# One quarter of the gate stage's input: transposed by DMA through DRAM in place of TensorE

## The chip, the cores and the metric

The kernel runs on one core of a Trainium2 chip. The core has five engines that run their own instruction streams and wait for one another by semaphores: TensorE (PE in the profile: matmuls and transposes into PSUM; PEld is its loading of the stationary operand), VectorE (DVE), ScalarE (ACT), GpSimd (POOL) and SyncE (SP), which here only issues DMAs. DMAs issued by SyncE and by GpSimd run on the same 16 DMA engines. The metric is the device time of one execution in microseconds. A measurement is the median of several executions.

## The reference

One layer of a transformer trunk on 512 tokens of width 2048, all in float32: a sliding-window attention mixer, then a gated embedding, then a norm. Cut to what matters here:

```python
x = x + swa_mixer(rmsnorm(x, norm_g), ...)      # attention, ends with (out * silu(gate)) @ w_out
emb = p @ ple_proj                              # [512, 256] @ [256, 2048]
g = sigmoid(rmsnorm(x, ple_norm) @ ple_gate)    # [512, 2048] @ [2048, 2048]
x = x + emb * g
return rmsnorm(x, final_g)
```

The change concerns the step from the second line's left side to the third: x, which lies with tokens on partitions, must be turned so that its 2048 columns lie on partitions, because a matmul contracts over partitions. The columns are scaled by `ple_norm` on the way. The mean square of each token enters later, as a scale of the sigmoid's input.

## The kernel before

Float32 products are made from three matmuls each (`mm3`, lines 126 to 128): both operands are split into a rounded high part and the rest, and high x high, low x high and high x low are added. The high part of a weight piece is a cast on ScalarE (line 729), the low part a subtraction on VectorE (line 730). So one weight piece of 128 x 1024 is loaded (L722, on SyncE; L709 on GpSimd where it is added to what is there), cast, subtracted, and then used by twelve matmuls.

The last two matrix products of the layer, the output projection (stage "o", with `w_out`) and the gate (stage "g", with `ple_gate`), are each made as seven products of half-size blocks instead of eight (a Strassen scheme; in the output stage one of the seven is itself made of seven smaller ones). `ORDER_OUT` = (1, 7, 6, 5, 3, 4) and `ORDER_PLE` = (2, 7, 1, 6, 5, 3, 4) give the order of the products. Each product p has two halves jj of its columns, and each half (a call of `unit`) four steps m: a step takes one weight piece, gives out a share of the list `later` (additions into x, squares), calls `todo()` and then `between(m)`, which handles the smaller products. The forms (sums of quarters of the left operand, split in high and low) of the next product are made beside the current one by the generator `nxt`; those of the first gate product by `ple_first`.

`x1[j]` is column block j (512 columns) of x, with tokens on partitions, t = 0 to 3 counting blocks of 128 tokens. `add_to_x` adds a product to a block and counts in `missing` how many additions are still due; with the last one it calls `squares(t, j)`. The blocks with t >= 2 and j >= 2, the lower right quarter of x, get their last addition from product 5.

`hT[g]` is column block g of the turned x: 128 partitions, 4 blocks of 128 columns, 512 tokens. `turn(kp, th, tag)` turns the column blocks 2kp and 2kp + 1 for one half th of the tokens: four TensorE transposes of 128 x 128 into one PSUM bank (L1023), then two multiplications by `ple_norm` on ScalarE into `hT` (L1026). There are 16 such turns. Twelve are spread over the steps of the last output product (p = 4), in this order: the columns 1024 to 2047 for tokens 256 to 511, the same columns for tokens 0 to 255, the columns 0 to 1023 for tokens 0 to 255. The last four (columns 0 to 1023, tokens 256 to 511) stand in the first gate product. The lower right quarter (`hT[2]` and `hT[3]`, tokens 256 to 511) is needed first by the forms of gate product 6, which are made beside product 1.

What sets the order: TensorE's and SyncE's instructions run as the program lists them; from the second gate product on those of all engines do. Before that, the order on ScalarE, VectorE and GpSimd is a scheduler's. SyncE's loads follow the rule in `Pieces.ahead`: a piece is asked for 6 pieces ahead in the output stage (from product 6 on), 3 or 4 in the gate stage, and each load waits in SyncE's queue until its buffer is free. `pT` (L1168), an operand of the embedding product, is loaded after the output stage into a buffer of the weight pieces, cast at L1169 and subtracted at L1170.

The `quarter` buffers (four of them) hold the attention gates first and `hT` afterwards. The tile `partial` (two buffers) holds intermediate results `s2` and `s7` of the gate stage.

Of the kernel before, what the change touches and what calls it, by code (L numbers as in the profile page):

```python
# [10 lines left out]

F32 = mybir.dt.float32
F32R = mybir.dt.float32r
AF = mybir.ActivationFunctionType
ALU = mybir.AluOpType
AX = mybir.AxisListType
# [4 lines left out]
P = 128  # L21
# [34 lines left out]
def trunk_kernel(ctx: ExitStack, tc: tile.TileContext, a: dict):  # L56
    nc = tc.nc
# [12 lines left out]
    pn = const.tile([P, KC], F32, name="pn")  # L70
# [8 lines left out]
    def quarter(name):  # L79
        return whole.tile([P, 4, S], F32, tag="quarter", name=name)  # L80
# [7 lines left out]
    class Weights:  # L88
# [15 lines left out]
        def _make(self, i):  # L104
            self.load(min(i + 2, len(self.srcs)))
            raw = self.raw[i]
            hi = wpool.tile([P, WE], F32R, tag="whi", name=f"whi{i}")
            lo = wpool.tile([P, WE], F32R, tag="wlo", name=f"wlo{i}")
            nc.scalar.copy(hi, raw)  # L109
# [48 lines left out]
    def run(gen):  # L158
        for _ in gen:
            pass  # L160
# [34 lines left out]
    for k in range(KC):  # L195
# [25 lines left out]
        h = room.tile([P, S], F32R, tag="ah", name=f"xh{k}")  # L221
# [41 lines left out]
        f, e = k == 0, k == KC - 1  # L263
# [18 lines left out]
        for part in "hl" if f else "lh":  # L282
            for t in range(NB):
                c = slice(t * P, (t + 1) * P)
# [6 lines left out]
        if 3 <= k < 3 + NB:  # L291
            t = k - 3
# [110 lines left out]
    for b in range(exact, BUCKETS):  # L403
        d = np.nonzero(bk == b)[0]
        if len(d):
            lo, n = P - 1 + int(d.min()), len(d)
# [130 lines left out]
    def turn(i):  # L537


        d, g = divmod(i, UNITS)  # L540
        pr = T.pop(i)
        pt = bank(f"pt{i}", "t")[:, :256]
        for u in range(2):
            nc.tensor.transpose(pt[:, u * P : (u + 1) * P], pr[:, u, :], ident)  # L544

        j, part = divmod(i, 2)
        if part == 0:
            own = None
            if g >= P // TQ:
                own = apool.tile([P, 2, S], F32R, tag="own", name=f"own{j}")  # L550
            PT[j] = apool.tile([P, 2, S], F32R, tag="r", name=f"r{j}"), own
        r, own = PT[j]
        rh, rl = (r[:, l].rearrange("p (h t u q) -> p t u h q", h=GROUP, t=2, u=2)[:, part] for l in range(2))
        src = pt.rearrange("p (u h q) -> p u h q", u=2, h=GROUP)
        nc.scalar.copy(rh, src)  # L555
        nc.vector.tensor_sub(rl, src, rh.bitcast(F32))  # L556
        yield
        b = j % 2
        flat = lambda v, rows: v[rows].rearrange("p l (h t q) -> p t (l h) q", h=GROUP, t=2)[:, part]
        if own is not None:  # L560
            rows = slice(0, P) if b else slice(0, HB)
            sign = -1 if b else 1
            nc.gpsimd.affine_select(  # L563
                out=flat(own, rows), in_=flat(r, rows).bitcast(F32), pattern=[[0, 2 * GROUP], [sign, TQ]],
                compare_op=ALU.is_ge, fill=0.0, base=(-HB - 1 if b else 0) + sign * part * TQ, channel_multiplier=-sign,
            )
        yield
        if own is not None:
            here, there = slice(HB, P), slice(0, HB)
            if not b:  # L570
                here, there = there, here
            nc.scalar.copy(flat(own, there)[:, :GROUP], flat(own, here)[:, GROUP:].bitcast(F32))
# [98 lines left out]
    for (nm, p), small in zip(SUMS, (7, 5, 6, 4, None, None)):  # L671
        for m in range(2 if small else 0):
            t = summed["small", small, m] = tc.dram_tile([P, WE], F32, name=f"small_{small}_{m}")
# [5 lines left out]
        for jj in range(2):  # L679
            for m in range(4):  # L680
                t = summed[nm, p, jj, m] = tc.dram_tile([P, WE], F32, name=f"{nm}_{p}_{jj}_{m}")
# [223 lines left out]
    for i in range(blocks + 3):  # L905

        before, softmax = softmax, scores(i) if i < blocks else iter(())
        turned = turn(i - 2) if 2 <= i < blocks + 2 else iter(())
# [48 lines left out]
    x1 = [x1s[:, j] for j in range(4)]  # L957
# [46 lines left out]
    def partial(nm):  # L1004
        return late.tile([P, 2, 2, 512], F32, tag="partial", name=nm, bufs=2)

    def squares(t, j):
        junk = late.tile([P, 512], F32, tag="junk", name=f"junk{j}_{t}", bufs=3)
        nc.scalar.activation(junk, x1[j][:, t, :], AF.Square, accum_out=ssq2[:, t, j : j + 1])

    hT = {}

    def turn(kp, th, tag):

        g = kp // 2
        if g not in hT:
            hT[g] = quarter(f"hT{g}")
        tp = bank(f"tp{kp}_{th}", tag)
        for n in range(2):
            k = 2 * kp + n  # L1020
            for tb in range(2):
                src = x1[k // 4][:, 2 * th + tb, (k % 4) * P : (k % 4 + 1) * P]
                nc.tensor.transpose(tp[:, (2 * n + tb) * P : (2 * n + tb + 1) * P], src, ident)  # L1023
        for n in range(2):
            k = 2 * kp + n
            nc.scalar.mul(hT[g][:, k % 4, th * 256 : th * 256 + 256], tp[:, n * 256 : n * 256 + 256], pn[:, k : k + 1])  # L1026
# [9 lines left out]
    def add_to_x(j, t, sign, ps):  # L1036
        xt = x1[j][:, t, :]
        if sign > 0:
            nc.vector.tensor_add(xt, ps, xt)
        else:  # L1040
            nc.vector.tensor_sub(xt, xt, ps)
        missing[j, t] -= 1
        if not missing[j, t]:
            squares(t, j)


    halves = [gates[2 + h][:, :, :256].rearrange("p k (r t) -> p r k t", r=2) for h in range(2)]
# [67 lines left out]
    turns = []  # L1115
# [7 lines left out]
    for n, p in enumerate(ORDER_OUT):  # L1123
        nxt = out_forms.steps(ORDER_OUT[n + 1]) if n < 5 else iter(())
        for jj in range(2):
            later.extend(held.pop(waiting.get((p, jj)), ()))
            calls = iter(range(4))

            def between(m):
                q = small_steps.get((p, jj, m))  # L1130
                if q is not None:
                    next(small_made.setdefault(q, small_form(q)))
                q = SMALL.get((p, jj), {}).get(m)
                if q is not None:
                    small(q)

            def todo():
                step = next(calls)
                part = x_at.get((p, jj, step))
                if part is not None:  # L1140
                    load_x(part, nc.sync)
                next(nxt, None)
                if p == 4:

                    for _ in range({0: 1, 1: 2, 2: 2, 3: 2, 5: 1, 6: 2, 7: 2}.get(4 * jj + step, 0)):
                        turn(*turns.pop(0), "o")
                    if jj:
                        next(ple_first, None)

            ps = unit(p, jj, at_out, out_forms, todo, between)  # L1150
            posts = [partial_of(add_y, p, jj, tb, ps[tb]) for tb in range(2)]
            if p == 1:
                held[p, jj] = posts
            else:
                later.extend(posts)
        run(nxt)
        if p == 3:
            nc.sync.dma_start(fg, a["final_g"].partition_broadcast(P))
        if p == 3:
            turns = [(kp, th) for kp0, th in ((4, 1), (4, 0), (0, 0)) for kp in range(kp0, kp0 + 4)]  # L1160
    run(ple_first)
    assert not turns

# [51 lines left out]
    turns = [(kp, 1) for kp in range(4)]  # L1215
# [36 lines left out]
    early = {(5, 0, 3): 0, (5, 1, 1): 1, (5, 1, 3): 2, (3, 0, 1): 3, (3, 0, 3): 4, (3, 1, 1): 5, (3, 1, 3): 6}  # L1252
# [10 lines left out]
    for n, p in enumerate(ORDER_PLE[:-1]):  # L1263
        if n == 1:

            ctx.enter_context(
                tc.manual_schedule(
                    engines={getattr(mybir.EngineType, v) for v in ("PE", "SP", "DVE", "Activation", "Pool")}
                )
            )  # L1270
        nxt = ple_forms.steps(ORDER_PLE[n + 1])
        for jj in range(2):
            calls = iter(range(4))

            def todo():
                k = early.get((p, jj, next(calls)))
                if turns:
                    turn(*turns.pop(0), "s")
                    if not turns:
                        nc.vector.tensor_reduce(ss2, ssq2, axis=AX.X, op=ALU.add)  # L1280
                        run(rsqrt_mean(rstd2, ss2, D, "r2"))
                    return
                next(nxt, None)
                if p == 2:
                    next(nxt, None)
                if k is not None:
                    split_last(k)

            ps = unit(p, jj, at_ple, ple_forms, todo)
            e = {}  # L1290
            if p in (1, 5, 3):
                w = B.get(at_ple[p, jj][3] + 1)
                for t in (0, 1) if p in (1, 3) else (2, 3):
                    e[t] = embed(t, w, "to"[jj])
            if (p, jj) != (3, 1):
                later.insert(0, partial_of(gate_later, p, jj, ps, e))
            if (p, jj) == (5, 1):
                later.extend(moved.pop())
        run(nxt)
# [5 lines left out]
    f = ple_forms.made[4]  # L1305
# [31 lines left out]
    g = block(0, 0, "s", "o")()  # L1337
# [12 lines left out]
    g = block(1, 0, "s", "t")()  # L1350
# [10 lines left out]
    g = block(0, 1, "p", "o")()  # L1361
# [13 lines left out]
    g = block(1, 1, "p", "t", slice(0, 256))()  # L1375
# [4 lines left out]
    n = done[3]  # L1380
# [87 lines left out]
```

## Time and profile before

| | us |
|---|---|
| median of 3 executions | 792.71 (791.97 to 794.43) |
| profiled execution | 792.22 |
| its span, first to last instruction | 790.4 |
| TensorE busy | 780.8 |
| VectorE busy | 590.9 |
| ScalarE busy | 517.3 |
| GpSimd busy | 141.0 |

The span is the time between the first and the last instruction of the profiled execution; the time of an execution lies somewhat above it. A busy time is the sum of the time in which an engine had an instruction in work. In 40 equal slices of the span (19.8 us each), the digits are tenths of busy time; PEclk is the clock that TensorE was granted, DMA the mean busy share of the 16 DMA engines:

```profile
PE   9999999999999999999999999999999999999995
...
ACT  6735368776877676766666654456699656656765
POOL 0030222333332313341333100000000120210000
PEclk9999999999999999999999999999999999999998
DMA  8787977999999989899878499667864996787633
```

The output stage ends and the gate stage begins about the 31st slice; the turns lie between 572.6 and 619 us.

### The profile page before, as it was taken

The numbers are of one execution on the slowest core, as the hardware profiler recorded it, in microseconds if no ns is written. First come the engines' busy times: TensorE is split into PE (matmuls) and PEld (weight loads), VectorE is DVE, ScalarE is ACT, GpSimd is POOL, SyncE is SP. The second block draws the span as 40 slices with busy tenths as digits, with TensorE's granted clock in tenths as the row PEclk, the third lists the DMA queues.
The fourth block names the chain that finished last, engine by engine and source line by source line (L and its number), as shares of the span: only waits on it lengthen the run. The fifth ranks groups of instructions, "written<-read, shape, count | busy, mean of one in ns | idle before, by whom it ended". The sixth has DMA issues, their size and how long they took to land.

```text
span 790.4 us, 11177 instructions
## 1 busy us (share of the span) xinstructions
PE 780.8 (99%) x3658; PEld 649.2 (82%) x3658; DVE 590.9 (75%) x1171; ACT 517.3 (65%) x1131; POOL 141.0 (18%) x252
## 2 busy tenths in 40 slices
PE   9999999999999999999999999999999999999995
PEld 7888888888888888888888888888888888888885
DVE  4537568877888678776777899778867757988896
ACT  6735368776877676766666654456699656656765
POOL 0030222333332313341333100000000120210000
PEclk9999999999999999999999999999999999999998
DMA  8787977999999989899878499667864996787633
GB/s 337 244 213 253 297 192 229 291 265 291 251 253 282 242 229 263 215 254 252 228 201 184 137 371 342 190 217 233 273 235 142 348 206 198 157 227 218 182 106 107
DMA packets 44618, 184.87 MB, mean 234 GB/s; under 512 B 6720, under 2 KB 7232, under 8 KB 39440
## 3 DMA queue, kind: packets, MB, share of 16 engines
q1 hardware_dynamic: 36480, 142.94, 52.0%
q0 software_dynamic: 8080, 41.22, 27.4%
q8 instruction: 29, 0.48, 0.2%
q14 instruction: 29, 0.24, 0.1%
HBM read 177.26 MB, written 62.97 MB: 304 GB/s over the span
## 4 chain that ended last, share of the span: by engine, by line
PE 98%; DMA 0%; DVE 0%; ACT 0%; issue 0%; ACTq 0%; SPq 0%; DVEq 0%
PE gps L126 7%; PE gps L127 7%; PE gps L128 7%; PE qps L126 7%; PE qps L127 7%; PE qps L128 7%; PE o L128 6%; PE g L128 6%; PE g L126 6%; PE o L126 6%; PE g L127 5%; PE o L127 5%; PE s L476 2%; PE o L584 2%; PE vps L286 2%; PE pt L544 2%
## 5 line engine op out<-in xcount | busy, mean ns | idle before, releaser
L730 DVE TENSOR_TENSOR blo<-braw,bhi 128x1024 fp32r<-128x1024 f32 x102 | 124.5, 1223 | 41.0 <-ACT bhi L729 40.5
L729 ACT CAST bhi<-braw 128x1024 fp32r<-128x1024 f32 x102 | 107.4, 1053 | 72.8 <-PE o L128 26.4
L126 PE MATMUL gps<-xh,whi 128*128 128x512 f32 x256 | 100.5, 393 | 0.0
L127 PE MATMUL gps<-xl,whi 128*128 128x512 f32 x256 | 100.0, 391 | 0.0
L128 PE MATMUL gps<-xh,wlo 128*128 128x512 f32 x256 | 99.8, 390 | 0.0
L126 PE MATMUL qps<-xh,whi 128*128 128x512 f32 x224 | 87.6, 391 | 0.0
L127 PE MATMUL qps<-xl,whi 128*128 128x512 f32 x224 | 87.5, 391 | 0.0
L128 PE MATMUL qps<-xh,wlo 128*128 128x512 f32 x224 | 87.2, 389 | 0.0
L110 DVE TENSOR_TENSOR wlo<-wraw,whi 128x1024 fp32r<-128x1024 f32 x60 | 74.3, 1239 | 13.1 <-ACT whi L109 12.4
L126 PE MATMUL g<-bhi,fhg 128*128 128x512 f32 x192 | 75.1, 391 | 0.0
L126 PE MATMUL o<-bhi,fho 128*128 128x512 f32 x192 | 74.8, 390 | 0.0
L128 PE MATMUL g<-bhi,flg 128*128 128x512 f32 x192 | 74.8, 389 | 0.0
L128 PE MATMUL o<-bhi,flo 128*128 128x512 f32 x192 | 74.7, 389 | 0.0
L127 PE MATMUL g<-blo,fhg 128*128 128x512 f32 x192 | 74.7, 389 | 0.0
L127 PE MATMUL o<-blo,fho 128*128 128x512 f32 x192 | 74.7, 389 | 0.0
L555 ACT CAST r<-pt 128x256 fp32r<-128x256 f32 x64 | 23.9, 373 | 74.6 <-PE pt L544 74.5
L556 DVE TENSOR_TENSOR r<-pt,r 128x256 fp32r<-128x256 f32 x64 | 27.1, 423 | 57.2 <-ACT r L555 56.9
L109 ACT CAST whi<-wraw 128x1024 fp32r<-128x1024 f32 x60 | 62.3, 1039 | 10.6 <-PE qps L127 5.9
L563 POOL TENSOR_SCALAR_AFFINE_SELECT own<-r 64x512 fp32r<-64x512 f32 (+1 forms) x48 | 34.4, 718 | 167.0 <-PE o L587 80.7
L491 POOL COPY t<-sinkb 128x2 f32<-128x2 f32 x64 | 41.2, 644 | 99.3 <-ACT pr L533 38.7
L128 PEld LDWEIGHTS gps<-xh,wlo 128*128 128x128 f32 x256 | 48.1, 188 | 10.3
L126 PEld LDWEIGHTS gps<-xh,whi 128*128 128x128 f32 x256 | 48.1, 188 | 8.9
(230 smaller groups left out, 1753.5 us busy)
## 6 DMA issues: line engine op xcount, KB each, us to landing
w_out<-in_w_out POOLq DMA_DIRECT2D x32, 512.0 KB, 8.1
wraw<-in_w_gate_in SPq DMA_DIRECT2D x32, 512.0 KB, 6.8
braw<-w_out SPq DMA_DIRECT2D x32, 512.0 KB, 4.7
wraw<-in_w_q SPq DMA_DIRECT2D x28, 512.0 KB, 7.3
braw<-in_ple_gate SPq DMA_DIRECT2D x24, 512.0 KB, 3.6
braw<-in_w_out SPq DMA_DIRECT2D x22, 512.0 KB, 4.3
xw<-in_first SPq DMA_DIRECT2D x14, 640.5 KB, 6.5
w_out<-in_w_out SPq DMA_DIRECT2D x16, 512.0 KB, 11.2
```

Of the source, the lines that this page charges most:

```text
L109: nc.scalar.copy(hi, raw)
L110: nc.vector.tensor_sub(lo, raw, hi.bitcast(F32))
L126: nc.tensor.matmul(ps, sh, mh, start=first, stop=False, skip_group_check=more)
L127: nc.tensor.matmul(ps, sh, ml, start=False, stop=False, skip_group_check=more)
L128: nc.tensor.matmul(ps, sl, mh, start=False, stop=last, skip_group_check=more)
L286: nc.tensor.matmul(v_ps[t], h[:, c], part_of(high_at, 256, 512), start=f, stop=e, skip_group_check=True)
L491: nc.gpsimd.tensor_copy(two(0, W + W - 1 if late else W, 1), sinkb[:, d : d + 1].unsqueeze(1).to_broadcast([P, 2, 1]))
L555: nc.scalar.copy(rh, src)
L556: nc.vector.tensor_sub(rl, src, rh.bitcast(F32))
L563: nc.gpsimd.affine_select(out=flat(own, rows), in_=flat(r, rows).bitcast(F32), pattern=[[0, 2 * GROUP], [sign, TQ]], compare_op=ALU.is_ge, ...
L729: nc.scalar.copy(hi, raw)
L730: nc.vector.tensor_sub(lo, raw, hi.bitcast(F32))
```

## The change

The lower right quarter of x no longer goes through TensorE. Its four blocks of 128 tokens x 512 columns go another way:

- `apart(t, j)`, called right after a block's squares: GpSimd copies the block, seen as 16 bit halves, so that the lower halves of a row come first and the upper halves behind them, into a `partial` tile, and a DMA of GpSimd's queue stores it in DRAM (`halves_of`).
- `cross(t, j)`, called at steps 1 and 3 of both halves of output product 4: SyncE issues one transposing DMA that reads those 256 rows of 512 halves and writes them into `hT[j]`, so that the two halves of each value meet again side by side.
- `crossed(kp)`, at the four steps of the first half of gate product 7: ScalarE multiplies the eight column blocks by `ple_norm` in place.

The four turns of that quarter are gone. The other eight turns of output product 4 keep their steps; steps 0 and 1 have none any more, and step 2 has one in place of two. The four turns in the first gate product stay.

```diff
+    def turned(g):
         if g not in hT:
             hT[g] = quarter(f"hT{g}")
+        return hT[g]
+
+    halves_of = [tc.dram_tile([2 * P, 2, 512], U16, name=f"halves_of{n}") for n in range(2)]
+    parts_of, crossings = [], []
+
+    def apart(t, j):
+
+        if not parts_of:
+            parts_of.append(partial("apart").rearrange("p a b c -> p (a b c)").bitcast(U16))
+        n = len(crossings)
+        to = parts_of[0][:, 1024 * n : 1024 * n + 1024].rearrange("p (h c) -> p h c", h=2)
+        nc.gpsimd.tensor_copy(to, x1[j][:, t, :].bitcast(U16).rearrange("p (c h) -> p h c", h=2))
+        nc.gpsimd.dma_start(halves_of[j - 2][(t - 2) * P : (t - 1) * P], to)
+        crossings.append((t, j))
+
+    def cross(t, j):
+
+        to = turned(j).rearrange("p k t -> p (k t)").bitcast(U16).rearrange("p (k t) -> p k t", k=4)
+        rows = halves_of[j - 2][(t - 2) * P : (t - 1) * P].rearrange("t h c -> (t h) c")
+        nc.sync.dma_start_transpose(to[:, :, t * 2 * P : (t + 1) * 2 * P], rows)
+
+    def crossed(kp):
+        for k in (2 * kp, 2 * kp + 1):
+            part = hT[kp // 2][:, k % 4, 256:]
+            nc.scalar.mul(part, part, pn[:, k : k + 1])
...
@@ def add_to_x
         if not missing[j, t]:
             squares(t, j)
+            if t >= 2 and j >= 2:
+                apart(t, j)
...
@@ todo of the output stage
                 if p == 4:
 
-                    for _ in range({0: 1, 1: 2, 2: 2, 3: 2, 5: 1, 6: 2, 7: 2}.get(4 * jj + step, 0)):
+                    if step % 2:
+                        cross(*crossings[2 * jj + step // 2])
+                    for _ in range({2: 1, 3: 2, 5: 1, 6: 2, 7: 2}.get(4 * jj + step, 0)):
                         turn(*turns.pop(0), "o")
...
         if p == 3:
-            turns = [(kp, th) for kp0, th in ((4, 1), (4, 0), (0, 0)) for kp in range(kp0, kp0 + 4)]
+            turns = [(kp, th) for kp0, th in ((4, 0), (0, 0)) for kp in range(kp0, kp0 + 4)]
...
@@ todo of the gate stage
-                k = early.get((p, jj, next(calls)))
+                step = next(calls)
+                k = early.get((p, jj, step))
+                if p == 7 and jj == 0:
+                    crossed(4 + step)
```

More of the change, by code (lines that the diff above doesn't have):

```diff
@@ L13 @@
 F32R = mybir.dt.float32r
+U16 = mybir.dt.uint16
 AF = mybir.ActivationFunctionType
@@ L1011, in trunk_kernel @@
     hT = {}
+    def turned(g):
+        if g not in hT:
+            hT[g] = quarter(f"hT{g}")
+        return hT[g]
[17 more added lines that the diff above has]
+            nc.scalar.mul(part, part, pn[:, k : k + 1])
     def turn(kp, th, tag):
         g = kp // 2
-        if g not in hT:
-            hT[g] = quarter(f"hT{g}")
+        turned(g)
         tp = bank(f"tp{kp}_{th}", tag)
```

## The prediction

> **What bounds the kernel now.** I read the page first: busy times, then the chain that ended last.
>
> ```profile
> span 790.4 us, 11177 instructions
> ...
> PE 780.8 (99%) x3658; PEld 649.2 (82%) x3658; DVE 590.9 (75%) x1171; ACT 517.3 (65%) x1131; POOL 141.0 (18%) x252
> ...
> PE 98%; DMA 0%; DVE 0%; ACT 0%; issue 0%; ACTq 0%; SPq 0%; DVEq 0%
> ```
>
> TensorE (PE) is the chain: 98% of it, and 790.4 - 780.8 = 9.6 us is all the idle time that it has. So a change gains what it takes out of PE's stream, and loses what makes PE wait. The stages around the edit, as stretches of the span (busy us of each engine, clock, DMA share, GB/s):
>
> ```profile
> 535.00:555.00 20.00, 20.00 (x90) 16.57 (x89) 16.72 (x19) 12.15 (x17) 0.00 (x0) 1.00 0.74 231
> ...
> 577.00:592.00 15.00, 15.00 (x80) 12.66 (x79) 10.60 (x13) 13.36 (x27) 0.00 (x0) 1.00 0.71 241
> 592.00:597.50 5.50, 5.50 (x28) 4.56 (x27) 4.64 (x7) 5.00 (x8) 0.00 (x0) 1.00 0.00 0
> ...
> 626.00:651.00 25.00, 25.00 (x112) 20.71 (x111) 13.53 (x13) 13.68 (x18) 6.90 (x8) 1.00 1.03 216
> ```
>
> PE (the second number) fills every stretch at full clock, even the one where DMA is saturated (share 1.03). GpSimd (POOL) has nothing to do from 451 to 626, and DMA stands still from 592 to 597.5.
>
> **What goes: 16 transposes on TensorE.** The transposes, by tile:
>
> ```profile
> L1023 PE MATMUL tp<-ident,x1s x64: 270/272/273, 572.6 to 617.9; 128*128 128x128 f32 x64
> L1026 ACT ACTIVATE hT<-tp,pn x32: 458/468/492, 574.3 to 619.1; 128x256 f32<-128x256 f32 x32
> ```
>
> One turn is 4 transposes; four turns go: the one at step 0, both at step 1, one of two at step 2 of the last output product (p = 4). The tempting sum is 16 x 0.272 = 4.35 us. But matmuls overlap, and what counts is from start to start:
>
> ```profile
> 572.32 0.40 PE L128 MATMUL o<-bhi,flo 128*128 128x512 f32 x1
> 572.56 0.60 PE L1023 MATMUL tp<-ident,x1s 128*128 128x128 f32 x4
> 572.91 0.48 PE L126 MATMUL small<-bhi,small_ah 128*128 128x512 f32 x1
> 573.23 0.39 PE L127 MATMUL small<-blo,small_ah 128*128 128x512 f32 x1
> 573.46 0.40 PE L128 MATMUL small<-bhi,small_al 128*128 128x512 f32 x1
> ...
> 577.12 1.03 PE L1023 MATMUL tp<-ident,x1s 128*128 128x128 f32 x8
> 577.91 0.47 PE L126 MATMUL small<-bhi,small_ah 128*128 128x512 f32 x1
> 578.22 0.39 PE L127 MATMUL small<-blo,small_ah 128*128 128x512 f32 x1
> ```
>
> Ordinary matmuls start 0.23 apart (573.23 to 573.46). Four transposes hold the stream for 0.35 and make the next step 0.32 instead of 0.23: 573.23 - 572.56 - 0.23 = 0.44 us. Eight cost 578.22 - 577.12 - 0.23 = 0.87. Removed: 0.44 (step 0) + 0.87 (step 1) + 0.44 (half of step 2, 4 x 0.11) = **1.75 us**, all of it on the chain. With them go 8 ScalarE (ACT) multiplications of at most 0.47 us; they come back later.
>
> **What comes on GpSimd: 4 copies, 4 stores.** A block is copied once its last addition is made, in product 5's wake:
>
> ```profile
> 527.38 1.28 DVE L1039 TENSOR_TENSOR x1s<-o,x1s 128x512 f32<-128x512 f32 x2
> ...
> 542.51 0.68 DVE L1039 TENSOR_TENSOR x1s<-o,x1s 128x512 f32<-128x512 f32 x1
> ```
>
> Two blocks are done by 528.7, the last of the four at 543.2. A GpSimd copy that sorts 1,024 halves per partition isn't in this trace. Bounds: 0.72 us, its 128x512 select, below, and four times that, 2.9 us, above, since its elements are small and strided; I take 1.4, near the select, which has half as many elements. An issue on its queue is 0.86, and 256 KB from it land in 5.0:
>
> ```profile
> 418.07 0.72 POOL L563 TENSOR_SCALAR_AFFINE_SELECT own<-r 128x512 fp32r<-128x512 f32 x1 [2.58 <-DVE r L556]
> ...
> 626.28 0.92 POOL L709 DMA_DIRECT2D grown<-in_ple_gate  x1 [174.05 <-DMA braw<-in_ple_gate]
> ```
> ```profile
> x1s<-s POOLq DMA_DIRECT2D x4, 256.0 KB, 5.0
> ```
>
> 543.2 + 1.4 + 0.9 + 5.0 = 550.5 for the last, at worst 552. Cost 0: GpSimd is idle there, and SyncE asks for the last block only after 580. If they took 30 us more, SyncE would stand at a crossing and the loads behind it would pay what the first rival below pays.
>
> **What comes on SyncE: 4 transposing DMAs.** The new calls stand in SyncE's order, and SyncE runs far ahead of PE. Its loads (L722) carry the order of the pieces, so each crossing can be placed:
>
> ```profile
> 568.58 0.32 SPq L722 DMA_DIRECT2D braw<-w_out  x1
> 571.51 0.33 SPq L722 DMA_DIRECT2D braw<-in_w_out  x1
> ...
> 577.38 2.63 SPq L722 DMA_DIRECT2D braw<-w_out  x2
> 580.07 1.38 SPq L722 DMA_DIRECT2D braw<-in_ple_gate  x3
> 581.49 1.09 SPq L1168 DMA_DIRECT2D pT<-in_pT  x1
> 597.60 9.62 SPq L722 DMA_DIRECT2D braw<-in_ple_gate  x4
> ```
>
> Loads are asked for 6 pieces ahead, so crossing 0 falls between 568.58 and 571.51, crossing 1 between the two loads of 577.38, crossing 2 before 580.07, crossing 3 before pT. Each waits for its halves (there by 552) and for the gate quarter that hT2 and hT3 reuse, last read for product 3's forms, which are made a whole product earlier: no wait at issue. Behind them queue the last piece of w_out, three pieces of ple_gate, pT, and then the load of 597.6, which waits for pT's buffer. I write T for the time by which one crossing delays what is behind it, issue and transfer together. pT is first to feel it:
>
> ```profile
> DMA to landing us min/median/max: 10.4/10.4/10.4
> ```
> ```profile
> 594.80 1.06 ACT L1169 CAST pTh<-pT 128x1024 fp32r<-128x1024 f32 x1
> 596.36 1.06 ACT L729 CAST bhi<-braw 128x1024 fp32r<-128x1024 f32 x1 [0.49 <-PE o L128]
> ```
> ```profile
> 597.49 1.22 DVE L730 TENSOR_TENSOR blo<-braw,bhi 128x1024 fp32r<-128x1024 f32 x1
> ```
> ```profile
> 601.52 0.48 PE L126 MATMUL o<-bhi,fho 128*128 128x512 f32 x1
> ```
>
> It lands at 581.5 + 10.4 = 591.9 and is cast at 594.80: 2.9 us of slack. ACT's next cast had 0.49 of idle time; its piece is finished by VectorE (DVE) at 598.7 and used at 601.52: 2.8 more. So the three crossings right ahead of pT may cost 2.9 + 0.5 + 2.8 = **6.2 us** together before PE stops, T = 2.07 each. The loads behind have more: the one of 597.6 is four pieces behind the piece of 601.52, that is 4 x 12 x 0.23 = 11 us and the turns between, about 614. Crossing 0 has 8 us to itself.
>
> No row shows a transposing DMA. Nearest rows:
>
> ```profile
> out<-x1s SPq DMA_DIRECT2D x14, 256.0 KB, 2.9
> ...
> rb<-rdram POOLq DMA_DIRECT2D x1, 256.0 KB, 7.2
> ...
> rdram<-rstd POOLq DMA_DIRECT2D x1, 2.0 KB, 10.6
> ```
>
> Lower end: 0.26 MB at the 241 GB/s that this stretch moves, 1.1 us (3.3 for three: no stall, and DMA's empty 592 to 597.5 takes it up). 2.9, the whole landing of a 256 KB store, would be 8.7 - 6.2 = 2.5 us of stall. Upper ends: 7.2, the 256 KB of broadcast rows; 10.6, a transfer cut into 4-byte pieces. A transfer of this size from contiguous rows is nearest the store's, of whose 2.9 much is latency that overlaps; I take T = 1.1 to 2, stall 0. A cost below zero is excluded: nothing leaves this queue.
>
> Two pages of the Trainium skill bear on T, and no run here shows either. "DMA: Bandwidth & Descriptors", section "Latency and other measured facts", gives 261 GB/s to a transposing DMA: an estimate of 1.0 us each, and the sum stays.
>
> **What comes on ACT: 8 multiplications in place,** two a step in the gate stage's second product (p = 7, jj = 0), from about 629; the negated forms of product 1 (L841), made beside it, date it:
>
> ```profile
> 629.10 1.06 ACT L729 CAST bhi<-grown 128x1024 fp32r<-128x1024 f32 x1 [1.67 <-PE g L128]
> 630.06 1.06 ACT L1223 COPY s<-g 128x512 f32<-128x512 f32 x2
> 631.01 0.64 ACT L841 ACTIVATE fhg<-hT 128x512 fp32r<-128x512 f32 x1
> 631.82 1.06 ACT L729 CAST bhi<-grown 128x1024 fp32r<-128x1024 f32 x1 [0.17 <-PE g L128]
> ```
>
> Bounds for the pair: 0 and 2 x 0.47 = 0.94. In the first step it pushes the cast of 631.82 by up to 0.77; that cast is for a piece two pieces (5.4 us) ahead and with VectorE's half needs 2.3, so 3 us are free, and later steps have idle time. Cost 0, at most those 0.77 without the cover. Their data landed some 40 us before; the form that reads them is made in product 1.
>
> **Sum:** -1.75 + 0 + 0 + 0. The profiled execution took 792.22 us (span 790.4, 1.8 around it): 790.47. It stands 0.49 under the median of 792.71; carried over, 790.96. About 0.3%, 2.4 us, is what a measurement of this kernel can tell from no change: **a gain of 0.22%, within it**.
>
> **Rivals.**
> *The crossings hold the queue (slower).* pT and the ple_gate pieces behind them come late, ACT stands at pT's cast with the weight casts behind it, and PE starves near 601. It decides from T = 2.07. With 7.2: 3 x 7.2 - 6.2 - 1.75 = +13.7, 806.4; with 4.0, +4.1, 796.8; with 10.6, 816.6. For it: a store through 2-byte columns is unlike any load here, and T is unknown. Against: the DMA gap, 0 GB/s, right behind. Chance 0.25, 0.13 of it past T = 4.
> Another page speaks for this rival: the Trainium skill's "VectorE: DVE Perf Modes", section "The three transpose paths", has 1309 ns for a 128x128 block of 16-bit values by DMA. A crossing is 8 such blocks; one after another, an estimate of 10.5 us each.
> *The transposes are worth their busy time (faster).* 4.35 us, 788.4. The start-to-start rows speak against it. Chance 0.08.
> *The gain is given back.* In 626 to 651, DMA share 1.03, the loads, not PE, could set the pace, and an earlier start only waits there: 792.7. Against: PE 25.00 of 25.00. Chance 0.09.
> *The forecast*: 0.58.
>
> **Numbers.** Predicted 791.0. The range from 788.4 (busy time counted in full) to 797 (T = 4) leaves 0.13 out, and the far ends of T with it. Faster by over 0.3% (under 790.3): 0.08, and 0.07 for the forecast, which lies 0.7 us from that bound, read a little low: 0.15. Slower (over 795.1): the first rival from T = 3.5, 0.22. Within: 0.51 of the forecast, 0.09, and 0.03 of the first rival: 0.63.
>
> **What would show it.** PE: 48 transposes, and p = 4 some 1.75 us shorter. SyncE: transposing DMAs at 569 to 581 with short issues; landing of pT by 595. ACT: pTh's cast not waiting for a DMA. Wrong if PE has idle time between 590 and 625, if SyncE's issues of the crossings take microseconds, or if ACT's new multiplications wait for a crossing.

## The result, and the profile after

| | before | changed kernel |
|---|---|---|
| median, us | 792.45 (13 executions) | 791.07 (790.47 to 792.05, 13 executions) |
| ratio | | 0.998, 95% interval 0.9972 to 0.9989 |
| span of the profiled execution, us | 790.4 | 789.3 |

One of the 13 executions before took 1606.03 us, for a reason that no record shows; without it the median is 792.36.

The change is worth 0.2%. The interval leaves 1 out, but the gain stays under the 0.3% that was set as what can be told from no change. Span and busy times of the changed kernel, then its chain that ended last, from its page:

```profile
span 789.3 us, 11171 instructions
...
PE 779.4 (99%) x3642; PEld 647.9 (82%) x3642; DVE 591.4 (75%) x1171; ACT 517.4 (66%) x1131; POOL 148.8 (19%) x260
...
PE 98%; ACT 1%; DVE 0%; DMA 0%; issue 0%; ACTq 0%; DVEq 0%
```

PE has 3,642 matmuls, 16 fewer, and is still 98% of the chain. Its busy time fell by 1.4 us, not by the 4.35 that 16 durations of 0.272 add up to. Its idle time, 789.3 - 779.4 = 9.9 us, was 9.6 before: something new makes it wait for a moment. Three stretches of the span (PE is the second number; clock, DMA share and GB/s are the last three):

```profile
577.00:592.00 15.00, 14.90 (x71) 12.04 (x71) 10.32 (x11) 11.59 (x22) 0.00 (x0) 1.00 0.59 161
592.00:597.50 5.50, 5.50 (x27) 4.52 (x26) 4.94 (x6) 5.01 (x8) 0.00 (x0) 1.00 0.68 270
626.00:651.00 25.00, 25.00 (x112) 20.72 (x111) 14.25 (x14) 17.03 (x28) 5.98 (x7) 1.00 1.05 230
```

From 577 to 592 PE is no longer full: 14.90 of 15.00. And DMA has moved: its share there fell from 0.71 to 0.59, and the stretch 592 to 597.5, in which it stood still, is at 0.68. Loads have been put off. The queue that issues them, SyncE's, by its timeline (start, us, what):

```profile
568.96 2.17 SPq L1036 DMA_TRANSPOSE hT<-halves_of  x1
...
582.82 2.20 SPq L1036 DMA_TRANSPOSE hT<-halves_of  x1
...
588.51 1.23 SPq L1036 DMA_TRANSPOSE hT<-halves_of  x1
...
596.77 1.23 SPq L1036 DMA_TRANSPOSE hT<-halves_of  x1
598.05 0.58 SPq L1201 DMA_DIRECT2D pT<-in_pT  x1
```

The crossings came at 569.0, 582.8, 588.5 and 596.8, not all by 581; pT is asked for at 598.05, not 581.5. Why, the timeline of ACT in the same execution shows (idle time before the instruction, and what ended it, in brackets):

```profile
581.97 0.83 ACT L1055 ACTIVATE hT<-tp,pn 128x256 f32<-128x256 f32 x2
...
586.39 0.62 ACT L847 CAST fhg<-hT 128x512 fp32r<-128x512 f32 x1 [2.58 <-DMA hT<-halves_of]
586.92 1.56 ACT L1055 ACTIVATE hT<-tp,pn 128x256 f32<-128x256 f32 x4
588.36 2.01 ACT L730 CAST bhi<-braw 128x1024 fp32r<-128x1024 f32 x2
...
595.92 0.83 ACT L1055 ACTIVATE hT<-tp,pn 128x256 f32<-128x256 f32 x2
```

Crossing 1 starts 0.02 us after the turn's two multiplications end (581.97 + 0.83 = 582.80), crossing 2 right after the next four (588.48), crossing 3 after two more (596.75). (The view of waits names weight casts, L730, for three crossings and a subtraction of DVE for one. It infers them; in four executions the multiplications end 0.02 to 0.03 us ahead of each of crossings 1 to 3.) The multiplications write the columns of tokens 0 to 255 of hT, a crossing writes columns of tokens 256 to 511 of the same tile: no byte is shared, yet the queue waits. Then ACT waits in turn: its cast for a form of the first gate product, which reads the columns of tokens 0 to 255, stands 2.58 us until crossing 1 has landed. Behind that cast ACT's order has four multiplications, 1.44 us from start to start, and only then the next two weight casts. What that costs PE is in DVE's and PE's timelines:

```profile
589.45 2.36 DVE L731 TENSOR_TENSOR blo<-braw,bhi 128x1024 fp32r<-128x1024 f32 x2 [1.05 <-ACT bhi L730]
```
```profile
590.25 0.39 PE L127 MATMUL small<-bhi,small_ah 128*128 128x512 f32 x1
590.73 0.50 PE L128 MATMUL small<-blo,small_ah 128*128 128x512 f32 x1
591.07 0.40 PE L129 MATMUL small<-bhi,small_al 128*128 128x512 f32 x1
```

The weight casts behind the waiting cast come late, blo with them, and the matmuls at 590.73 and 591.07 start 0.48 and 0.34 after the one ahead instead of 0.23: 0.25 + 0.11 = 0.36 us. So the theory after the result was: 1.75 us saved, less 0.36 lost to an order between instructions that share a tile.

### The profile page after: what moved, and what is told of

Its sections match the earlier page's. It is cut to its first block, busy times and chain, and to the rows that moved or that the text cites. A ratio compares the mean times of both kernels' runs of the same rounds, so it can differ in the third digit from the quotient of the medians.

```text
span 789.3 us, 11171 instructions
## 1 busy us (share of the span) xinstructions
PE 779.4 (99%) x3642; PEld 647.9 (82%) x3642; DVE 591.4 (75%) x1171; ACT 517.4 (66%) x1131; POOL 148.8 (19%) x260
## 4 chain that ended last, share of the span: by engine, by line
PE 98%; ACT 1%; DVE 0%; DMA 0%; issue 0%; ACTq 0%; DVEq 0%
PE gps L127 7%; PE gps L128 7%; PE gps L129 7%; PE qps L127 7%; PE qps L128 7%; PE qps L129 7%; PE g L129 6%; PE g L127 6%; PE g L128 6%; PE o L129 5%; PE o L128 5%; PE o L127 5%; PE s L477 2%; PE o L585 2%; PE vps L287 2%; PE pt L545 2%
## 5 line engine op out<-in xcount | busy, mean ns | idle before, releaser
L730 ACT CAST bhi<-braw 128x1024 fp32r<-128x1024 f32 x102 | 107.2, 1052 | 71.9 <-PE o L129 24.2
```

## The experiments

To see terms smaller than the scatter of the whole time, I measured one stage of each profiled execution: from the first matmul of output product 4 to the first of the gate stage, both in PE's timeline. Before:

```profile
569.83 0.39 PE L126 MATMUL o<-bhi,fho 128*128 128x512 f32 x1
...
605.15 0.48 PE L126 MATMUL g<-bhi,fhg 128*128 128x512 f32 x1
```

The stage is 35.32 us. In the changed kernel it is 603.75 - 569.80 = 33.95: 1.37 shorter, which is 1.75 - 0.36 with 0.02 left over. Three executions with the change's order in this stage (the change, after_again, muls_x3) lie between 33.82 and 34.03, the six without PE's gap and without extra work within 0.03. The runs, with the same difference:

| run | what | time, us | ratio (95%) | stage, us |
|---|---|---|---|---|
| before | | 792.0 to 792.5 | 1 | 35.32 |
| the change | | 791.07 | 0.9980 (0.9972 to 0.9989) | 33.95 |
| after_again | the change, once more | 791.32 | 0.9986 (0.9978 to 0.9995) | 34.03 |
| own_tile | crossings into a tile of their own | 790.44 | 0.9977 (0.9967 to 0.9987) | 33.52 |
| own_again | the same, once more | 790.63 | 0.9976 (0.9967 to 0.9985) | 33.53 |
| early | crossings a product earlier | 790.69 | 0.9981 (0.9972 to 0.9990) | 33.52 |
| plain | DMA without transposing (the quarter stays unturned) | 790.74 | 0.9978 (0.9969 to 0.9987) | 33.55 |
| twice | before, four turns doubled | 793.75 | 1.0019 (1.0010 to 1.0028) | 37.03 |
| own_tile_x2 | own_tile, every crossing twice | 793.29 | 1.0020 (1.0010 to 1.0029) | 35.75 |
| own_tile_x3 | own_tile, every crossing three times | 798.15 | 1.0071 (1.0057 to 1.0084) | 39.78 |
| muls_x3 | the change, 16 more ACT instructions | 794.29 | 1.0031 (1.0018 to 1.0043) | 33.82 |
| six | six blocks by DMA, one turned too early | 789.90 | 0.9970 (0.9959 to 0.9981) | 33.52 |
| six_b | six blocks, turned later | 789.55 | 0.9964 (0.9951 to 0.9978) | 33.52 |

**own_tile: does sharing a tile make the wait?** The crossings land in a tile that nothing else writes; ACT's multiplications bring them into hT.

```diff
 def cross(t, j):
-    to = turned(j)....bitcast(U16)...
+    if not landed:
+        landed.append(partial("landed"))
+    to = landed[0][:, j - 2]....bitcast(U16)...
...
-        part = hT[kp // 2][:, k % 4, 256:]
-        nc.scalar.mul(part, part, pn[:, k : k + 1])
+        part = landed[0][:, k // 4 - 2]...[:, k % 4 * 256 : k % 4 * 256 + 256]
+        nc.scalar.mul(hT[kp // 2][:, k % 4, 256:], part, pn[:, k : k + 1])
```

> The crossings land in a tile of their own (a partial buffer that is free then) and the multiplications by ple_norm carry them from there into hT; all else as in the changed kernel. Theory (the crossings and the turns order one another because they share a tile, though not a byte): the four crossings issue near 569, 577.5, 580 and 581.5 us, no cast of a form waits for a crossing, PE has no gap near 590, and the first gate matmul starts at 605.15 - 1.75 = 603.4 (603.75 in the changed kernel). Ratio to before 0.9978. Rival (the transfers themselves make the weights late): a gap of PE of about 0.35 us or more between 585 and 605 remains, first gate matmul at 603.75 or later.

SyncE's timeline of own_tile:

```profile
569.27 1.55 SPq L1038 DMA_TRANSPOSE landed<-halves_of  x1
...
577.34 1.29 SPq L1038 DMA_TRANSPOSE landed<-halves_of  x1
...
583.65 2.84 SPq L1038 DMA_TRANSPOSE landed<-halves_of  x1
586.53 0.93 SPq L1203 DMA_DIRECT2D pT<-in_pT  x1
```

The crossings no longer follow the multiplications, pT goes out at 586.53, and ACT's cast of the quarter waits for no DMA. The same stretch as above:

```profile
577.00:592.00 15.00, 15.00 (x74) 12.48 (x73) 10.93 (x13) 12.90 (x24) 0.00 (x0) 1.00 1.13 294
```

PE is full again, 15.00 of 15.00, although DMA is now saturated here (share 1.13). The stage is 35.32 - 33.52 = 1.80 shorter than before, 0.43 shorter than the change's. The repeats (own_again, after_again) give 33.53 and 34.03; PE stands 0.47 us at the same matmul in after_again. The whole times differ by 0.6 to 0.7 us in both pairs, the intervals overlap: the trace tells the two kernels apart, the ratios don't.

> own_tile once more, beside the changed kernel and six_b on one chip: 0.36 us under the changed kernel if its one gap is all that tells them apart, ratio 0.9977.

> The changed kernel on the same chip: ratio 0.998 (0.9972 to 0.9989 at first); the gap of PE near 590, behind a form's cast that waits for a crossing, is there again if it comes of the program's order and not of one execution.

**early: the same tile, at another time.** The crossings go into hT, but in product 3, before any turn has written it.

```diff
+                if p == 3 and jj == 1:
+                    cross(*crossings[step])
...
-                    if step % 2:
-                        cross(*crossings[2 * jj + step // 2])
```

> The crossings go into hT as in the changed kernel, but at the four steps of the second half of output product 3, ahead of every turn. Theory (order within the shared tile): they are first in that order, so they wait for no turn, and they have landed before the first form is cast: no gap of PE, first gate matmul near 603.4, ratio 0.9978. Rival (the transfers themselves make the weights late): the gap moves with them, to about 560 to 580, and the first gate matmul is at 603.75 or later.

They were issued from 551.13 to 560.39, pT at 581.11, and PE has no gap: 33.52 again. So the crossings cost PE nothing where they don't meet the turns in one tile.

**plain: is it the transposition?** The same bytes, issued at the same places, moved by an ordinary DMA. GpSimd's copy leaves the halves together, and the quarter stays unturned, so this isn't the same layer.

```diff
-        nc.gpsimd.tensor_copy(to, x1[j][:, t, :].bitcast(U16).rearrange("p (c h) -> p h c", h=2))
+        nc.gpsimd.tensor_copy(to, x1[j][:, t, :].bitcast(U16).rearrange("p (h c) -> p h c", h=2))
...
-    rows = halves_of[...].rearrange("t h c -> (t h) c")
-    nc.sync.dma_start_transpose(to[:, :, t * 2 * P : (t + 1) * 2 * P], rows)
+    rows = halves_of[...].rearrange("t h (k c) -> t (h k) c", k=2)
+    nc.sync.dma_start(to[:, :, t * 2 * P : (t + 1) * 2 * P], rows)
```

> The same four DMAs with the same bytes, places and destination, not transposing (the halves stay together, rows of 512 bytes; the lower right quarter of the gate's input is x unturned). If the wait comes of the shared tile whatever the DMA, they too issue near 583, 588.5 and 597 and the gap near 590 stays, time as the changed kernel (0.998). If it comes of the transposing DMA alone, they issue near 577.5, 580 and 581.5 and the first gate matmul is near 603.4. In both cases this gives the price of transposing on the queue: issue on SyncE 0.3 to 0.5 us against 1.2 to 2.2, landing about 3 us against 3.4.

The waits of its SyncE queue (us in total, times, longest us), then ACT's timeline:

```profile
SPq L1036 <- ACT hT L1055: 10.6, 3, 5.8
```
```profile
586.65 0.62 ACT L847 CAST fhg<-hT 128x512 fp32r<-128x512 f32 x1 [2.51 <-DMA hT<-halves_of]
587.18 1.05 ACT L730 CAST bhi<-braw 128x1024 fp32r<-128x1024 f32 x1
588.13 1.55 ACT L1055 ACTIVATE hT<-tp,pn 128x256 f32<-128x256 f32 x4
```

The waits are there without any transposing DMA. They come from the order that the program keeps between instructions on one tile, not from the transposition. Yet PE had no gap here (33.55), so the expectation that the gap stays with the wait was missed. The stand of ACT is as long as in the change, 2.51 against 2.58, and ends at the same place in the stage: 16.5 us after its first matmul against 16.6. What differs is ACT's order behind it: here a weight cast goes ahead of the four multiplications, in the change behind them. With that DVE makes blo from 588.26, in the change from 589.45, and PE has it in time. So in plain the wait costs PE nothing; in the change, after_again and muls_x3 it meets the order with the multiplications first. Without their 1.44 us ahead of it, the change's blo would be made from about 588.0 to 589.2, by estimate from these rows, and the matmul that started at 590.73 was due at 590.48. Why the order differs no run shows, and none has that order without the wait. Both kernels' crossings by tile, first the change's, then plain's (issue min/median/max in ns; landing in us):

```profile
L1036 SPq DMA_TRANSPOSE hT<-halves_of x4: 1233/1703/2200, 569.0 to 596.8; - x4
...
DMA to landing us min/median/max: 3.3/3.4/6.7
```
```profile
L1036 SPq DMA_DIRECT2D hT<-halves_of x4: 530/546/620, 569.3 to 596.7; - x4
...
DMA to landing us min/median/max: 2.9/3.3/5.4
```

Whether the order is kept for the tile as a whole, or because its parts are seen once as 32 bit and once as 16 bit elements, these runs don't tell apart.

**twice: what is a turn worth?** The kernel before, with the four turns that the change removes done twice.

```diff
-        for n in range(2):
+        for n in [0, 1] * (2 if kp >= 4 and th else 1):
```

> The kernel before, with the 16 transposes of the lower right quarter made twice into the same bank (the second ones are extra work). Start-to-start price: first gate matmul 1.75 us later (606.9), ratio 1.0022. Busy-time price: 4.35 us later (609.5), ratio 1.0055.

The stage grew by 37.03 - 35.32 = 1.71 us. Taking the 16 transposes away gave 1.80 in own_tile and early, adding 16 takes 1.71: 0.11 us each, on both sides of the forecast's 1.75. A busy time of 0.272 each would have been 4.35.

**own_tile_x2, own_tile_x3: when do the crossings starve PE?** Each crossing is followed by one or two more of the same rows, into the tile apart, whose contents aren't needed any more.

```diff
         nc.sync.dma_start_transpose(to[...], rows)
+        for _ in range(1):
+            nc.sync.dma_start_transpose(again, rows)
```

(range(2) in own_tile_x3.)

> As own_tile, and each crossing issued a second time into a spent buffer, so that T, what a crossing delays, doubles. In own_tile pT was issued 586.5 and landed by 593, its cast ran at 593.2, and PE had no gap. The prediction's bound: PE stops when pT is cast more than some 3.3 us later than planned. Theory (the bound holds): the second set adds some 6 us of issues ahead of pT, pT lands about 598, 1.5 to 3 us of PE are lost near 600, first gate matmul 605 to 606.5, ratio 0.9995 to 1.001. Rival (more cover than the prediction counted, the empty DMA stretch takes it all): no gap, first gate matmul 603.6, ratio 0.9978.

> As own_tile, each crossing issued three times, the third behind the landing of the second (same destination), so that T is some 8 to 10 us. Theory (the prediction's first rival, with its price 3T - 6.2): pT lands 20 us or more later than before, the weight casts stand behind its cast, PE loses 12 to 22 us near 600, ratio 1.015 to 1.028. Rival (loads behind have cover of their own, since SyncE runs some 20 us ahead of PE): PE loses under 6 us, ratio under 1.006.

In own_tile_x2 pT is issued at 593.98 instead of 586.53. ACT's timeline, then PE's:

```profile
597.73 1.05 ACT L1208 CAST pTh<-pT 128x1024 fp32r<-128x1024 f32 x1 [4.71 <-DMA pT<-in_pT]
598.68 0.83 ACT L1061 ACTIVATE hT<-tp,pn 128x256 f32<-128x256 f32 x2
599.41 1.99 ACT L730 CAST bhi<-braw 128x1024 fp32r<-128x1024 f32 x2
```
```profile
600.50 0.50 PE L127 MATMUL o<-bhi,fho 128*128 128x512 f32 x1 [0.28 <-ACT bhi L730]
601.83 0.50 PE L128 MATMUL o<-blo,fho 128*128 128x512 f32 x1 [0.82 <-DVE blo L731]
```

This is the forecast's first rival, link by link: pT late, ACT standing 4.71 at its cast, the weight cast behind it late, PE standing at 600.5 and 601.8. The stage is 2.23 longer than own_tile's. But pT landed at 597.7, 5.8 after the 591.9 of before, and by the forecast's bound PE had 6.2 to spare. About 3.6 was left. Most of the difference is the change itself: with 16 transposes gone, PE comes to the matmul that stood at 601.52 in before 1.80 us sooner after the start of the stage (29.89 in own_tile, 31.69 before), so that of 6.2 only 4.4 remain. The rest is order: between pT's cast and the next weight cast stand two of the turn's multiplications, 0.73 from start to start, which in before stand behind that weight cast. DVE makes pTl and an addition to x1s before it comes to blo at 600.56; since bhi is there at about 600.46, that adds some 0.1:

```profile
598.82 1.23 DVE L1209 TENSOR_TENSOR pTl<-pT,pTh 128x1024 fp32r<-128x1024 f32 x1 [4.27 <-ACT pTh L1208]
599.96 0.68 DVE L1074 TENSOR_TENSOR x1s<-small,x1s 128x512 f32<-128x512 f32 x1
```

6.2 - 1.80 - 0.73 - 0.1 is the 3.6 that was left. The expectation for this run held (pT at 598, 1.5 to 3 us lost), but for a ratio of 1.0020 where at most 1.001 was expected.

With three, the stage is 6.26 longer. Here pT is issued at 609.76, and its cast has moved behind the start of the gate stage; what ACT waited for ahead of that was a weight piece that stood behind the crossings. ACT's timeline, PE's, and the windows of that stretch:

```profile
604.07 1.04 ACT L730 CAST bhi<-braw 128x1024 fp32r<-128x1024 f32 x1 [5.19 <-DMA braw<-in_ple_gate]
...
615.71 1.05 ACT L1208 CAST pTh<-pT 128x1024 fp32r<-128x1024 f32 x1 [4.56 <-DMA pT<-in_pT]
```
```profile
608.07 1.97 PE L1058 MATMUL tp<-ident,x1s 128*128 128x128 f32 x8 [5.27 <-ACT hT L1061]
```
```profile
608.00:612.00 4.00, 3.93 (x14) 3.44 (x15) 2.94 (x4) 3.15 (x8) 0.00 (x0) 0.50 0.56 110
612.00:616.00 4.00, 4.00 (x19) 3.29 (x18) 0.00 (x0) 0.29 (x1) 0.00 (x0) 0.86 0.97 347
```

PE's transposes stand 5.27 us for ACT's multiplications, which are queued behind that cast, and then PE runs at a clock of 0.50 (the number third from the end): the whole time is 7.7 us over own_tile's, more than the stall. The first 48 matmuls of the gate, with the transposes between, take 14.38 us to the start of the next, where own_tile's take 12.76. ACT's other wait, 4.56 us for pT, costs nothing: from 612 to 616 PE is busy 4.00 of 4.00. The forecast's formula, what goes beyond 6.2 us of pT's lateness, would have said some 18, for a pT that is there at 615.7, some 24 after the 591.9 of before. Neither expectation held: the theory's 12 to 22 us are far off, and 6.26 us and 1.0071 lie somewhat over the rival's 6 and 1.006. The formula priced the wrong transfer: pT's cast stands later in ACT's order where pT is issued later, the weight pieces are needed when PE comes to them.

**muls_x3: is ACT's cover real?** The change, with two copies behind each of the eight multiplications.

```diff
             nc.scalar.mul(part, part, pn[:, k : k + 1])
+            for _ in range(2):
+                nc.scalar.copy(part, part)
```

> The changed kernel, with two further copies in place on ScalarE behind each of the eight multiplications by ple_norm (16 more instructions of some 0.5 us between 629 and 640). Theory (ScalarE's casts run two pieces ahead, 3 us free, and 0.6 us a step are idle): 16 x 0.46 = 7.4 us more in 11 us of time that is 94% full, so casts come some 6 us late and PE loses 2 to 4 us near 640; with the eight alone there is room. Rival (the room is larger, casts not on the path): no gap, ratio 0.998.

In the changed kernel the pair stands like this on ACT:

```profile
629.61 0.92 ACT L1041 ACTIVATE hT<-hT,pn 128x256 f32<-128x256 f32 x2
```

0.92 us a pair, and PE is full from 626 to 651. With the copies, in muls_x3, PE is not (630 to 640, 640 to 650):

```profile
630.00:640.00 10.00, 9.65 (x44) 7.67 (x43) 4.60 (x5) 9.68 (x21) 1.70 (x2) 1.00 0.92 177
640.00:650.00 10.00, 8.48 (x33) 5.89 (x34) 5.25 (x6) 9.31 (x17) 2.55 (x3) 1.00 0.80 129
```

By the starts of PE's matmuls, what goes beyond 0.23 between two, it lost 0.62, 1.28 and 1.30 us at 639, 643 and 647, where it waited for blo: 3.2 in all, and the time is 3.2 over the change's. ACT is busy 9.68 of 10.00. The eight multiplications of the change are free, 16 more of their kind cost 0.2 each.

**six, six_b: two more blocks by DMA.** On own_tile; blocks of column quarter 0 cross too, so that 8 more transposes leave PE in the gate stage.

```diff
-            if t >= 2 and j >= 2:
+            if t >= 2 and j != 1:
                 apart(t, j)
...
+                if (p, jj, step) == (2, 0, 0):
+                    cross(*crossings[4])
+                    cross(*crossings[5])
```

six takes turns 2 and 3 first, which turns one block of x ahead of the last addition to it, so that it isn't the same layer. six_b takes them later, behind that addition:

```diff
-    turns = [(kp, 1) for kp in range(4)]
+    turns = [
+        lambda: None,
+        lambda: crossed(0),
+        lambda: (crossed(1), turn(2, 1, "s")),
+        lambda: turn(3, 1, "s"),
+    ]
```

> As own_tile, and a quarter of the remaining turns go the same way: the blocks j = 0, t = 2 and 3 (columns 0 to 511) are copied, stored and crossed too, issued at the first step of the first gate product, and the turns of kp = 0 and 1 there become multiplications in steps 2 and 3. 8 more transposes leave TensorE. Theory (start-to-start price, 0.11 us each, and cover on all other engines): 0.88 us under own_tile, ratio 0.9966. Rival (the stretch from 600 on, with the DMA queue saturated, has no cover for a crossing): the load of the next pieces or the forms of product 7 come late, a gap of PE between 605 and 630, ratio 0.9977 or more.

> As six, with the turn of kp = 2 behind the last addition to its block (in six it read one block of x an addition early): of the four steps the first is empty, then crossed(0), crossed(1) with the turn of kp = 2, and the turn of kp = 3. Theory (0.11 us for each of 8 more transposes, cover elsewhere): 0.88 us under own_tile in the same call, ratio 0.9966. Rival (no cover behind 600): a gap of PE between 605 and 630, no faster than own_tile.

The stage doesn't show what they save, since their turns lie behind its end. The gate stage does. From the start of its first matmul to that of its 193rd, transposes not counted, there are 45.51 us in the kernel before and in own_again (603.10 to 648.61), and 44.57 in six and six_b (603.15 to 647.72 in six_b): 0.94 for eight transposes, 0.12 each, and no gap of PE between 605 and 630. The rival, no cover behind 600, is refuted. six_b's 789.55 is 1.08 us under own_again's 790.63. With 0.9964 it is the fastest of all, though its interval reaches to 0.9978 and overlaps the change's.

## Why the prediction was right

The time was forecast as 791.0, and is 791.07. Within it, step by step:

- **The transposes, 1.75 us: right.** 1.71 when added, 1.80 when removed without side effects, 0.11 each by start to start. The rival of the busy time, 4.35, is refuted by the same runs.
- **GpSimd, cost 0: right.** By tile, copies and stores:

```profile
L1028 POOL COPY apart<-x1s x4: 1037/1310/2038, 528.1 to 544.3; 128x1024 uint16<-128x1024 uint16 x4
L1029 POOL DMA_DIRECT2D halves_of<-apart x4: 542/551/564, 531.1 to 545.7; - x4
...
DMA to landing us min/median/max: 2.7/4.4/5.2
```

A copy was taken as 1.4 us and has a median of 1.31, with one of 2.04; the last store was issued at 545.7 and landed by 545.7 + 5.2 = 550.9, 18 us ahead of the first crossing.
- **SyncE: "no wait at issue" was wrong, the cost 0 nearly right.** I asked when the tile's bytes had last been read and found them free. I didn't ask what else is written to that tile meanwhile: crossings 1 to 3 waited for multiplications into its other quarter, and ACT's cast waited for crossing 1. With the order that ACT has behind that cast in this kernel, it cost 0.36 us on PE, the only term of the sum that was missed. In own_tile and early both the wait and the gap are gone. plain shows that the wait isn't the transposition's, and that it costs nothing where ACT makes a weight cast first.
- **T, 1.1 to 2 us: right as a time on the queue, too long for what came behind it.** Without the wait, in own_tile, three crossings moved pT's issue from 581.49 to 586.53, 1.7 us each. pT landed 6.3 us later, at 592.8, 0.9 after before's 591.9. So by the forecast's own definition, issue and transfer together, a crossing delayed pT by 0.3, under the range. What took up the rest wasn't DMA's idle stretch, as forecast: in own_tile it stays nearly empty,

```profile
592.00:597.50 5.50, 5.50 (x28) 4.54 (x27) 5.50 (x6) 4.95 (x8) 0.00 (x0) 1.00 0.14 37
```

with a DMA share of 0.14, while from 577 to 592 the share rose from 0.71 to 1.13 and pT took 6.3 us to land, not 10.4. The kernel as changed put pT later still, 598.05, and it landed 4.7 later at 602.7, not by 595. That did no harm only because ACT's order in this kernel has its cast (L1202) later, at 603.11, without a wait.

- **The bound of 6.2 us: too wide,** by own_tile_x2 some 3.6. The slack was read from the timeline of before and not lessened by the 1.75 that the change itself takes out ahead of that place; by the prediction's own terms it was 6.2 - 1.75 = 4.45, or T = 1.48 for three crossings, and the first rival's prices, 3T - 6.2 - 1.75, are 1.75 too low. The 1.7 that a crossing delayed pT's issue lies past 1.48; the forecast was spared since pT landed only 0.9 late in own_tile.
- **The first rival, the crossings hold the queue: didn't happen, and is real.** It took twice the crossings to see it. The 1309 ns for a 128x128 block of 16 bit values, which the Trainium skill states in "VectorE: DVE Perf Modes", section "The three transpose paths", and from which I had estimated 10.5 us for 8 blocks, doesn't add up over the blocks of one DMA: all eight landed 3.4 us (median) after their issue. The 261 GB/s that the Trainium skill gives for a transposing DMA in "DMA: Bandwidth & Descriptors", section "Latency and other measured facts", and from which I had estimated 1.0 us, is no price for the queue: one crossing held it for 1.23 us or more.
- **ACT's multiplications, cost 0: right,** 0.92 a pair where at most 0.94 was taken, and muls_x3 shows how near the edge they lie.
- **The gain is given back at 626 to 651: refuted.** DMA's share is 1.05 there and PE is busy 25.00 of 25.00.

Of the signs that I had named as speaking against me, two came: SyncE's issues did take microseconds (1.23 to 2.20), harmlessly, since what stood behind them had time; and PE did stand between 590 and 625, for 0.36 us. That the median came within 0.1 of the forecast is partly luck: the loss of 0.36 wasn't in the sum, and the median before, 792.71 when the forecast was made, was 792.45 beside the changed kernel, 0.26 lower. The two nearly cancel; executions of this kernel scatter by 1.6 us.

## What to carry to other kernels

Price work that leaves a full pipeline by starts, not by durations: 16 instructions of 0.272 us were worth 1.75 us, and adding them again is a cheap way to measure it. When a DMA is moved into a tile that other engines are writing, count it as ordered with all of them, even where no byte is shared, as here, and try a tile of its own. And when a slack is read from the timeline of before, take off what the change itself brings forward, and look at the order on the engine again: mine was 6.2 us on paper and some 3.6 on the chip, 1.80 of the difference from the first and 0.73 from the second.

## What the runs showed of the hardware

**A transposing DMA holds its issuing queue.** 256 KB took 1.23 to 2.84 us of SyncE's queue in the change and own_tile, and up to 3.76 in own_tile_x2, where crossings stood behind each other; the same bytes in an ordinary DMA took 0.53 to 0.62 (plain). An ordinary issue isn't always short either: 1.36 us for a load of 512 KB right behind a crossing in plain. Landing hardly differs, 3.4 against 3.3 us in the median, where DMA has room; in own_tile, with DMA's share at 1.13, it was 5.6 to 8.0. The packets on the change's page:

```profile
DMA packets 49162, 186.97 MB, mean 237 GB/s; under 512 B 11008, under 2 KB 11520, under 8 KB 43984
```

Before it were 6,720 under 512 B, 4,288 fewer. plain, with the same stores and no transposing DMA, has 6,848, so some 1,040 small packets belong to each crossing: 256 KB in pieces of about 256 B.

**PE's clock falls after a stand.** In own_tile_x3, after 5.27 us without a matmul, the clock was 0.50 from 608 to 612, and matmuls started 0.43 us apart instead of 0.23, so here the stall cost more than itself. The Trainium skill, "TensorE: Matmul & The Clock Gate", section "Part 1: The HAM clock gate", says that TensorE's clock is halved after an idle window of about 3.4 us; this trace agrees, 0.50 after 5.27. The stalls of 0.36 to 1.3 us in the other runs left it at 1.00.
